# A hybrid decoder layer in fp32r on one core: where the attention of the later token tiles stands among the steps of the FFN

## The chip, the cores and the metric

One NeuronCore of a Trainium2 chip runs the whole program. The metric is device time in microseconds of one execution. The engines are named as in the profile: PE (TensorE matmul), PEld (its weight loads), DVE (VectorE), ACT (ScalarE), POOL (GpSimd) and SP (SyncE, which here issues every DMA).

## The reference, cut to what matters

One layer over 2048 positions with 1024 channels, all in float32:

```python
h = rmsnorm(x, attn_pre_norm);  qkv = h @ w_qkv
# group A: 4 heads of differential softmax attention (two maps, bias, causal) -> 512 columns
# group B: 8 heads of stick-breaking attention, 64 wide:
z = q @ k.T * 0.125
log_beta = log_sigmoid(z);  log_1mb = where(strict, log_sigmoid(-z), 0)
between = lax.cumsum(log_1mb, axis=3, reverse=True) - log_1mb
a = where(strict, exp(log_beta + between), 0);  o = rmsnorm(a @ v, sb_norm)
x = x + rmsnorm(concat(A, B) @ w_o, attn_post_norm)
h = rmsnorm(x, ffn_pre_norm)
u = causal_depthwise_conv(h @ w_up, conv_w, conv_b)     # 3 taps, 2 x 2816 columns
gate, val = split(u)
x = x + rmsnorm((gelu(gate) * val) @ w_down, ffn_post_norm)
```

## The kernel before

**Split arithmetic.** Every fp32 operand of a matmul is split into a high part rounded to fp32r and the rest; a product is three matmuls (high by high, high by low, low by high). A weight tile is split once on chip: `split` makes the high part on ACT or DVE (L477, L476) and the low part on POOL or DVE (L478, L480). Split w_up and w_down tiles are stored to DRAM (`wud`, `wdd`) and loaded again in split form for later token tiles. w_o is split for token tile 0 without a store, split again for tile 1 and stored (`wod`), and loaded in split form (512 KB a tile instead of 256 KB) for tiles 2 and 3.

**Stages.** First come the q/k/v projection in four passes and the differential attention. Then, for four token tiles of 512 positions, the stick-breaking attention (`sb_stream`) runs beside the rest of the projection and beside the FFN of earlier token tiles. The attention is a stream of 80 units: 8 for token tile 0, 16 for tile 1, 24 for tile 2 and 32 for tile 3. A unit is one head, one token tile and one 512-wide chunk of keys; `front` does its four row blocks (a matmul `z` L997, two sigmoids on ACT L1003 and L1005, one scan on DVE L1011, one product on POOL or DVE L1015 and L1017), and `tstep` transposes (L1029), splits (`hi` L485, `lo` L1036) and multiplies by v (L1052). So every unit has four scans, 320 in all.

The FFN of token tile t is `ffn_head(t)` (44 `up` steps of 24 matmuls, L1298, each with its convolution, and three of four rounds of `down`, L1351) and `ffn_tail(t)`: the output projection of the next tile `wo(t+1)` (L1218), the last round of `down`, and `h2(t+1)`, which transposes the normalised rows (L1274) into the operand `fh` of the next `up`. Between the last matmul of `wo(t+1)` and the first `up` of tile t+1 lies a chain for each of four row blocks: scale and square the projection (L1234, L1236), the reciprocal root on POOL (L402), add the residual loaded into one of two `xr` buffers (L1250), store x1 (L1253), square it (L1255), scale it (L1258), transpose (L1274), make `fh` (L1276 on ACT, L1278 on DVE). The end of `down` adds its partial sums (L1365), squares (L1373), scales (L1385), adds x1, loaded again from DRAM through the same two `xr` buffers (L1387 on POOL or L1389 on DVE), and stores the output.

**The order.** `Plan` lists the operations with a priority: the planned time `plan.now` at which the step that issues them was written, less a lead. `run` then walks through a model of the engines and always takes, for each engine that is free, the ready operation of lowest priority value whose buffers are free. What comes out is one fixed order for each engine. `merge` mixes two streams of steps in proportion to their matmul cost, and `until(sb, t, n)` hands out the attention up to the n-th unit of token tile t. Nothing keeps an operation of later priority from going first when it is ready and the earlier one is not. Weights are asked for ten tiles ahead (`AHEAD`), into five buffers `W`.

The last lines of `layer_kernel` set the mix:

```python
run(merge(until(sb, 1, 2), qkv_steps(3, 2, 8)))
ffn_switch()
run(merge(until(sb, 1, 5), wo(0)))
run(merge(until(sb, 1, 8), h2(0)))
head = list(ffn_head(2))
run(merge(until(sb, 2, 4), ffn(0)))
run(merge(until(sb, 3, 8), ffn(1)))
run(merge(until(sb), head[:-5]))
run(chain(head[-5:], ffn_tail(2), ffn(3)))
```

Of the kernel before, what the change touches and what calls it, by code (L numbers as in the profile page):

```python
# [276 lines left out]
def layer_kernel(  # L277
# [18 lines left out]
    x1d = [dram.tile([P, D], F32, name=f"x1d{i}") for i in range(NB)]  # L296
    wud = dram.tile([2 * NFT * 2, P, 1024], F32, name="wud")
    wdd = dram.tile([NFT * 2, P, 1024], F32, name="wdd")
    wod = dram.tile([KD * 2, P, 1024], F32, name="wod")
    fd = dram.tile([4, 384], F32, name="fd")  # L300

    ident = const.tile([P, P], F32, name="ident")
# [852 lines left out]
    def weight(n):  # L1155
        kind, a, b = key = jobs[n]
        w = buf("W")
        flat = lambda: f32(w.t).rearrange("p a n -> p (a n)")
        home = {"u": wud, "d": wdd, "o": wod}[kind][a * 2 + b if kind != "o" else b * 2 + a]
        if key in wstore:  # L1160
            wbufs[n] = w, (load(flat, home, 1 << 19, (w,), (wstore[key],), lead=0.0, what="wload"),)
            return
        raw = buf("raw2")
        if kind == "u":
            src = up_src[:, b * 4:(b + 1) * 4, a * P:(a + 1) * P]
            rv = lambda: raw.t.rearrange("p (k n) -> p k n", k=4)
        else:
            src = w_down[0, a * P:(a + 1) * P, b * 512:(b + 1) * 512] if kind == "d" else \
                wo_src[:, b, a * 512:(a + 1) * 512]
            rv = lambda: raw.t  # L1170
        o = load(rv, src, 1 << 18, (raw,), lead=0.0, what="wraw")
        ds = split(lambda: raw.t, lambda: w.t[:, 0, :], lambda: w.t[:, 1, :], 512, (o,), (raw, w), 0.0)

        first = key not in wseen
        wseen.add(key)
        if not first or (kind == "u" and b == 0) or (kind == "d" and a % 2 == 0):
            wstore[key] = op(SPE, 0, lambda: nc.sync.dma_start(home, flat()), ds, (w,), 0, 1 << 19, "wstore")
        wbufs[n] = w, ds

# [15 lines left out]
    def wo(t):  # L1195
        st = {}

        def begin():
            st["mix"] = []
            for k in range(KD):  # L1200
                b = buf("fh")
                assert len(mixs[k, t]) == (2 if k < 4 else 1)
                st["mix"].append((b, load(lambda b=b: f32(b.t), mixd[t][k], 1 << 19, (b,), mixs[k, t], lead=20e3,
                                          what="mixload")))

        def part(h, k, js):
            if (h, k) not in st:
                st[h, k] = take("o", h, k)
            w, wd = st[h, k]
            mb, ml = st["mix"][k]  # L1210
            for j in js:
                if k == 0:
                    st["ps", h, j] = buf("pf")
                ps = st["ps", h, j]

                def go(j=j, ps=ps):
                    for n, (a, b) in enumerate(((0, 0), (0, 1), (1, 0))):
                        nc.tensor.matmul(ps.t, mb.t[:, a, j * P:(j + 1) * P], w.t[:, b, :],  # L1218
                                         start=(k == 0 and n == 0), stop=(k == KD - 1 and n == 2))
                prev = st.get((h, j, "last"))  # L1220
                st[h, j, "last"] = op("PE", 3 * c_mm(512), go, [ml, *wd] + ([prev] if prev else []), (ps, mb, w),
                                      what="wo")
                if k == KD - 1:
                    evac(h, j, ps, st[h, j, "last"])

        def evac(h, j, ps, last):
            if h == 0:
                x1b[t, j] = buf("x1")
                st["ss", j] = small("ws"), []
            x1 = x1b[t, j]  # L1230
            ss, sq = st["ss", j]
            junk = buf("junk")
            xh = lambda c: x1.t[:, c * 512:(c + 1) * 512]
            sq.append(op("DVE", c_dvp(512), lambda: nc.vector.tensor_tensor(  # L1234
                xh(h), ps.t, gain_t[:, h * 512:(h + 1) * 512], ALU.mult), (last, mem["ga"]), (ps, x1)))
            sq.append(op("ACT", c_act(512, True), lambda: nc.scalar.activation(  # L1236
                junk.t[:, 0:512], ps.t, AF.Square, accum_out=ss.t[:, h:h + 1]), (last,), (ps, junk, ss)))
            if h == 0:
                return
            b = 4 * t + j  # L1240
            s2 = small("ws")
            o = op("DVE", 70, lambda: nc.vector.tensor_tensor(ss.t[:, 2:3], ss.t[:, 0:1], ss.t[:, 1:2], ALU.add), sq,
                   (ss,))
            r, o = rs_ops(lambda: ss.t[:, 2:3], D, 1, (o,), (ss,), "ws")
            os_ = []
            for c in range(2):
                xb = buf("xr")
                lx = load(lambda xb=xb: xb.t, x2[b * P:(b + 1) * P, c * 512:(c + 1) * 512], 1 << 18, (xb,), lead=20e3,
                          what="xload")
                os_.append(op("DVE", c_dvs(512), lambda c=c, xb=xb: nc.vector.scalar_tensor_tensor(  # L1250
                    xh(c), xh(c), r.t[:, 0:1], xb.t, ALU.mult, ALU.add), (o, lx), (x1, r, xb)))
            flat = lambda: x1.t
            x1store[b] = op(SPE, 0, lambda: nc.sync.dma_start(x1d[b], flat()), os_, (x1,), 0, 1 << 19, "x1store")  # L1253
            junk2 = buf("junk")
            o = op("ACT", c_act(D, True), lambda: nc.scalar.activation(  # L1255
                junk2.t, flat(), AF.Square, accum_out=s2.t[:, 0:1]), os_, (x1, junk2, s2))
            r2, o = rs_ops(lambda: s2.t[:, 0:1], D, 1, (o,), (s2,), "ws")
            xdone[t, j] = op("DVE", c_copy(D), lambda: nc.vector.tensor_scalar(  # L1258
                flat(), flat(), r2.t[:, 0:1], None, ALU.mult), (o, x1store[b]), (x1, r2))

        yield 0.0, begin
        for h in range(2):
            for k, js in rank(KD):
                yield 3 * len(js) * c_mm(512), lambda h=h, k=k, js=js: part(h, k, js)

    def h2(t):

        def step(k):
            ps, hb = buf("pf"), buf("fh")
            xs = [x1b[t, j] for j in range(4)]  # L1270

            def tr():
                for j in range(4):
                    nc.tensor.transpose(ps.t[:, j * P:(j + 1) * P], xs[j].t[:, k * P:(k + 1) * P], ident)  # L1274
            o = op("PE", 436, tr, [xdone[t, j] for j in range(4)], (*xs, ps), what="h2T")
            o1 = op("ACT", c_act(512) + 95, lambda: nc.scalar.activation(  # L1276
                hb.t[:, 0, :], ps.t, AF.Identity, scale=g_ffn[:, k:k + 1]), (o, mem["gffn"]), (ps, hb))
            o2 = op("DVE", c_dvp(512), lambda: nc.vector.scalar_tensor_tensor(  # L1278
                hb.t[:, 1, :], ps.t, g_ffn[:, k:k + 1], f32(hb.t[:, 0, :]), ALU.mult, ALU.subtract), (o1,), (ps, hb))
            h2b[t][k] = hb, (o1, o2)  # L1280

        for k in range(KD):
            yield 436, lambda k=k: step(k)

    ysv, halod, gts, yas, yss = {}, {}, {}, {}, {}

# [47 lines left out]
    def down(t, r, h):  # L1334
# [24 lines left out]
        def evac(j, ps, last):  # L1359
# [19 lines left out]
                   (ss,))  # L1379
            rr, o = rs_ops(lambda: ss.t[:, 2:3], D, 1, (o,), (ss,), "ws")  # L1380
            for c in range(2):
                yc, xb = yas[t, c, j][0], buf("xr")
                cs = slice(c * 512, (c + 1) * 512)
                lx = load(lambda xb=xb: xb.t, x1d[rb][:, cs], 1 << 18, (xb,), (x1store[rb],), lead=20e3, what="x1load")
                oc = op("DVE", c_dvs(512), lambda yc=yc, cs=cs: nc.vector.scalar_tensor_tensor(  # L1385
                    yc.t, yc.t, rr.t[:, 0:1], mem["gain"][:, cs], ALU.mult, ALU.mult), (o, mem["gf"]), (yc, rr))
                oc = op("POOL", c_pool(512), lambda yc=yc, xb=xb: nc.gpsimd.tensor_tensor(  # L1387
                    yc.t, yc.t, xb.t, ALU.add), (oc, lx), (yc, xb)).alt(
                    "DVE", c_dvs(512), lambda yc=yc, xb=xb: nc.vector.tensor_tensor(yc.t, yc.t, xb.t, ALU.add))  # L1389
                op(SPE, 0, lambda yc=yc, cs=cs: nc.sync.dma_start(out2[rb * P:(rb + 1) * P, cs], yc.t), (oc,), (yc,),  # L1390
                   0, 1 << 18, "out")

# [3 lines left out]
    def ffn_head(t):  # L1396
        for r, (a, b) in enumerate(ROUNDS):
# [3 lines left out]
            if r + 1 < len(ROUNDS):  # L1401
                for h in range(2):
                    yield from down(t, r, h)

    def ffn_tail(t):
        if t + 1 < NTT:
            yield from wo(t + 1)
        for h in range(2):
# [49 lines left out]
    op(None, 0, sb_open, users("k", "v", "q", "thi", "tlo", "mo", "ot", "os", "sq", "mix", "sm", "z", "o", "w", "a"))  # L1458
    sb = sb_stream()
    plan.slack = 2500.0  # L1460
    run(merge(until(sb, 1, 2), qkv_steps(3, 2, 8)))
    ffn_switch()
    run(merge(until(sb, 1, 5), wo(0)))
    run(merge(until(sb, 1, 8), h2(0)))
    head = list(ffn_head(2))
    run(merge(until(sb, 2, 4), ffn(0)))
    run(merge(until(sb, 3, 8), ffn(1)))
    run(merge(until(sb), head[:-5]))
    run(chain(head[-5:], ffn_tail(2), ffn(3)))
    plan.run()  # L1470
# [36 lines left out]
```

## Time and profile before

| | |
|---|---|
| median of 2 runs | 3154.66 us (3153.62 to 3155.71) |
| the profiled execution | 3157.89 us, span 3156.1 us |
| mean granted TensorE clock | 0.980 |
| PE busy | 3006.2 us (95%) |
| DVE busy | 2125.1 us (67%) |
| ACT busy | 1451.7 us (46%) |
| POOL busy | 649.4 us (21%) |
| DMA | 630.47 MB, 200 GB/s over the span |

The span is the time from the first to the last instruction of the profiled execution; the device time has a little around it. Busy shares are of the span. A matmul's own duration is longer than the distance between two of them, so PE can read as wholly busy while it doesn't run at its densest; the number of matmuls in a stretch tells more than its busy time.

### The profile page before, as it was taken

The page shows a single profiled execution, that of the slowest core. Times are in us where ns is not written, and L with a number is a line of the kernel's source. Part 1 is how long each engine was busy: PE and PEld are TensorE (multiplying, and loading weights), DVE is VectorE, ACT ScalarE, POOL GpSimd, SP SyncE. Part 2 cuts the span into 40 slices and gives each one's busy share as a digit, 9 for nine tenths or more (in the row PEclk, how much of TensorE's full clock was granted, in tenths as well). Part 3 has the DMA queues.
Part 4 walks back from the last instruction along what each step waited for, and adds up shares of the span by engine and source line. Part 5 has one row for each costly group of instructions (what it writes and reads, how often), then busy time and mean ns, then how long its engine had stood idle before and what let it go on. Part 6 is the DMA issues. An engine that isn't in the chain of part 4 may idle for free.

```text
span 3156.1 us, 47203 instructions
## 1 busy us (share of the span) xinstructions
PE 3006.2 (95%) x16840; PEld 2590.9 (82%) x16840; DVE 2125.1 (67%) x4273; ACT 1451.7 (46%) x2861; POOL 649.4 (21%) x831
## 2 busy tenths in 40 slices
PE   7999999999998899999889999998999999899997
PEld 7899999999997688888777887876888888678885
DVE  4657877679577676676586878778767777352334
ACT  4434545445344555455355556454655555222112
POOL 1011001002022332222331333333233222100000
PEclk9999999999999899999999999999999999999998
DMA  7776748565576555656676666676655555665665
GB/s 250 254 221 187 212 138 243 152 205 166 161 221 207 170 183 184 197 184 201 233 239 227 210 215 209 210 236 204 208 177 178 173 172 191 217 214 193 194 193 161
DMA packets 344256, 630.47 MB, mean 200 GB/s; under 512 B 29680, under 2 KB 200404, under 8 KB 335828
## 3 DMA queue, kind: packets, MB, share of 16 engines
q1 hardware_dynamic: 344020, 627.45, 62.4%
q8 instruction: 133, 2.18, 0.3%
q14 instruction: 103, 0.84, 0.1%
HBM read 449.07 MB, written 178.26 MB: 199 GB/s over the span
## 4 chain that ended last, share of the span: by engine, by line
PE 77%; DVE 10%; DMA 3%; ACT 2%; issue 2%; POOL 1%; SPq 0%; POOLq 0%; DVEq 0%; ACTq 0%
PE pf L1298 28%; PE pf L1351 13%; PE g L623 9%; PE g L620 5%; PE pf L1218 4%; PE o L1052 3%; PE z L726 3%; PE zt L997 3%; PE zt L1029 3%; DVE gm L1011 2%; PE t L744 2%; PE o L906 1%; PE o L911 1%; PE o L905 1%; DVE ya L1385 1%
## 5 line engine op out<-in xcount | busy, mean ns | idle before, releaser
L1298 PE MATMUL pf<-fh,W 128*128 128x512 f32 x4224 | 1041.7, 395 | 0.1
L1298 PEld LDWEIGHTS pf<-fh,W 128*128 128x128 f32 x4224 | 784.7, 189 | 164.7 <-DVE fh L1278 0.4
L1351 PE MATMUL pf<-W,gt 128*128 128x512 f32 x2112 | 532.3, 396 | 11.5 <-DVE x L1234 3.8
L1351 PEld LDWEIGHTS pf<-W,gt 128*128 128x128 f32 x2112 | 390.0, 189 | 97.0 <-DVE ya L1365 6.8
L623 PE MATMUL g<-hT,big 128*128 128x256 f32 x3072 | 446.8, 288 | 11.0 <-DVE st L642 5.7
L1015 POOL TENSOR_TENSOR be<-be,gm 128x512 f32<-128x512 f32 (+3 forms) x218 | 292.1, 1350 | 725.2 <-DVE gm L1011 419.6
L623 PEld LDWEIGHTS g<-hT,big 128*128 128x128 f32 x3072 | 407.3, 193 | 22.3 <-DVE st L642 7.7
L1011 DVE TENSOR_TENSOR_SCAN gm<-gm,gm 128x513 f32<-128x513 f32 x192 | 277.2, 1463 | 34.5 <-ACT gm L1003 33.6
L1036 DVE TENSOR_TENSOR lo<-zt,hi 128x512 fp32r<-128x512 f32 (+1 forms) x320 | 192.5, 605 | 119.6 <-ACT hi L485 118.0
L1309 DVE SCALAR_TENSOR_TENSOR fy<-pf,cw,fy 128x511 f32<-128x511 f32 x176 | 131.2, 745 | 210.1 <-ACT fy L1305 206.5
L485 ACT CAST hi<-zt 128x512 fp32r<-128x512 f32 (+3 forms) x250 | 130.2, 523 | 258.4 <-PE zt L1029 256.0
L1305 ACT ACTIVATE fy<-pf,cw 128x512 f32<-128x512 f32 x176 | 137.0, 778 | 210.6 <-PE pf L1298 210.6
L620 PE MATMUL g<-big,hT 128*128 128x256 f32 x1536 | 227.1, 289 | 5.3 <-DVE st L662 1.9
L620 PEld LDWEIGHTS g<-big,hT 128*128 128x128 f32 x1536 | 206.3, 194 | 11.3 <-DVE st L662 2.2
L1003 ACT ACTIVATE gm<-zt 128x512 f32<-128x512 f32 (+2 forms) x320 | 172.8, 540 | 82.6 <-PE zt L1000 44.5
L477 ACT CAST W<-raw 128x512 fp32r<-128x512 f32 x193 | 119.6, 623 | 190.7 <-PE pf L1298 68.9
L1029 PE MATMUL zt<-ident,be 128*128 128x128 f32 x1088 | 178.3, 279 | 24.5 <-POOL be L1015 8.9
L402 POOL TENSOR_TENSOR sm<-sm,neghalf 128x2 f32<-128x2 f32 (+1 forms) x72 | 71.3, 991 | 618.4 <-DVE sm L400 590.0
L1218 PE MATMUL pf<-W,fh 128*128 128x512 f32 x768 | 191.0, 402 | 7.7 <-DMA fh<-mixd 6.9
L997 PE MATMUL zt<-k,q 128*128 128x512 f32 (+3 forms) x640 | 183.1, 381 | 12.8 <-DVE lo L1036 8.8
L480 DVE TENSOR_TENSOR W<-raw,W 128x512 fp32r<-128x512 f32 x150 | 114.1, 763 | 117.6 <-ACT W L477 112.8
L1029 PEld LDWEIGHTS zt<-ident,be 128*128 128x128 f32 x1088 | 138.4, 144 | 62.6 <-POOL be L1015 10.3
(158 smaller groups left out, 4590.2 us busy)
## 6 DMA issues: line engine op xcount, KB each, us to landing
W<-wud SPq DMA_DIRECT2D x220, 512.0 KB, 3.9
W<-wdd SPq DMA_DIRECT2D x110, 512.0 KB, 4.4
hT<-hd SPq DMA_DIRECT2D x48, 1024.0 KB, 5.6
wud<-W SPq DMA_DIRECT2D x88, 512.0 KB, 4.1
raw<-in_w_up_dram SPq DMA_DIRECT2D x132, 256.0 KB, 3.3
q<-qd SPq DMA_DIRECT2D x128, 256.0 KB, 4.8
wdd<-W SPq DMA_DIRECT2D x44, 512.0 KB, 4.1
k<-kd SPq DMA_DIRECT2D x80, 256.0 KB, 3.7
```

Of the source, the lines that this page charges most:

```text
L620: nc.tensor.matmul(ps.t[:, cs], hk[:, b, c * P:(c + 1) * P], wv[:, a, k, :], start=first, stop=last)
L623: nc.tensor.matmul(ps.t[:, cs], wv[:, a, k, c * P:(c + 1) * P], hk[:, b, :], start=first, stop=last)
L997: nc.tensor.matmul(ps.t[:, 0:w], q.t[:, l, jj * P:(jj + 1) * P], kt.t[:, 0:w], start=(l == 0), stop=(l == 1 and not diag))
L1003: o1 = op("ACT", c_act(w), lambda: nc.scalar.activation(gm.t[:, 0:w], ps.t[:, 0:w], AF.Sigmoid, scale=-1.0), (o,), (gm, ps), what="sig").t ...
L1011: nc.vector.tensor_tensor_scan(gr, gr, gr, 1.0 if cb is None else cb[0].t[:, 0:1], ALU.mult, ALU.bypass)
L1015: o = op("POOL", c_pool(w), lambda: nc.gpsimd.tensor_tensor(be.t[:, 0:w], be.t[:, 0:w], gm.t[:, 1:w + 1], ALU.mult), (o1, o2), (be, gm), w ...
L1029: nc.tensor.transpose(ps.t[:, jj * P:(jj + 1) * P], rows[jj][0].t[:, kb * P:(kb + 1) * P], ident)
L1036: ol = op("DVE", c_dvp(n), lambda: nc.vector.tensor_tensor(lo.t[:, sl], ps.t[:, sl], f32(hi.t[:, sl]), ALU.subtract), (oh,), (ps, hi, lo), ...
L1218: nc.tensor.matmul(ps.t, mb.t[:, a, j * P:(j + 1) * P], w.t[:, b, :], start=(k == 0 and n == 0), stop=(k == KD - 1 and n == 2))
L1298: nc.tensor.matmul(ps.t, wv[:, a, k % 4, :], h2b[t][k][0].t[:, b, :], start=(k == 0 and i == 0), stop=(k == KD - 1 and i == 2))
L1305: o1 = op("ACT", c_act(512) + 95, lambda: nc.scalar.activation(y.t, ps.t, AF.Identity, scale=sc(2), bias=sc(3)), (last, *mem["cw"]), (ps, ...
L1351: nc.tensor.matmul(ps.t, gt.t[:, x, j * P:(j + 1) * P], w.t[:, y, :], start=(i == 0 and n == 0), stop=(m == b - 1 and n == 2))
```

## The change

Four edits of one kernel.

- `ffn_tail(0)` and `ffn_tail(1)` are run by themselves, with no attention units mixed in; they were mixed with attention as parts of `ffn(0)` and `ffn(1)`.
- The attention units are shared out anew. Up to the end of the named step there were 10 units (projection), 13 (`wo(0)`), 16 (`h2(0)`), 28 (`ffn(0)`), 56 (`ffn(1)`) and 80 (`ffn_head(2)`). Now there are 10 at the end of the projection's tile 5, 14 at its end, 19 (`wo(0)`), 24 (`h2(0)`), 40 (`ffn_head(0)`), 60 (`ffn_head(1)`) and 80 (`ffn_head(2)`).
- The operations that `evac` of `wo` issues and those of each `h2` step get a priority 30 us earlier.
- w_o is split from its raw form for every token tile; `wod`, its stores and its loads in split form are gone. For the last token tile the four x1 blocks are loaded whole into the four `x1` buffers at the start of `ffn_tail(3)`, instead of in halves through `xr`.

```diff
-        home = {"u": wud, "d": wdd, "o": wod}[kind][a * 2 + b if kind != "o" else b * 2 + a]
+        home = None if kind == "o" else {"u": wud, "d": wdd}[kind][a * 2 + b]
...
-        if not first or (kind == "u" and b == 0) or (kind == "d" and a % 2 == 0):
+        if kind != "o" and (not first or (kind == "u" and b == 0) or (kind == "d" and a % 2 == 0)):
             wstore[key] = op(SPE, 0, lambda: nc.sync.dma_start(home, flat()), ds, (w,), 0, 1 << 19, "wstore")
...
                 if k == KD - 1:
+                    now, plan.now = plan.now, plan.now - 30e3
                     evac(h, j, ps, st[h, j, "last"])
+                    plan.now = now
...
+        def soon(k):
+            now, plan.now = plan.now, plan.now - 30e3
+            step(k)
+            plan.now = now
+
         for k in range(KD):
-            yield 436, lambda k=k: step(k)
+            yield 436, lambda k=k: soon(k)
...
-                lx = load(lambda xb=xb: xb.t, x1d[rb][:, cs], 1 << 18, (xb,), (x1store[rb],), lead=20e3, what="x1load")
+                if t == NTT - 1:
+                    xb, lx = xlast[j]
+                    xv = lambda xb=xb, cs=cs: xb.t[:, cs]
+                else:
+                    xb = buf("xr")
+                    xv = lambda xb=xb: xb.t
+                    lx = load(xv, x1d[rb][:, cs], 1 << 18, (xb,), (x1store[rb],), lead=20e3, what="x1load")
...
+    xlast = []
+
+    def load_last():
+        for j in range(4):
+            rb = 4 * (NTT - 1) + j
+            xb = buf("x1")
+            xlast.append((xb, load(lambda xb=xb: xb.t, x1d[rb], 1 << 19, (xb,), (x1store[rb],), what="x1load")))
+
     def ffn_tail(t):
+        if t == NTT - 1:
+            yield 0.0, load_last
...
-    run(merge(until(sb, 1, 2), qkv_steps(3, 2, 8)))
+    run(merge(until(sb, 1, 2), qkv_steps(3, 2, 6)))
+    run(merge(until(sb, 1, 6), qkv_steps(3, 6, 8)))
     ffn_switch()
-    run(merge(until(sb, 1, 5), wo(0)))
-    run(merge(until(sb, 1, 8), h2(0)))
+    run(merge(until(sb, 1, 11), wo(0)))
+    run(merge(until(sb, 2, 0), h2(0)))
+    run(merge(until(sb, 2, 16), ffn_head(0)))
+    run(ffn_tail(0))
+    run(merge(until(sb, 3, 12), ffn_head(1)))
+    run(ffn_tail(1))
     head = list(ffn_head(2))
-    run(merge(until(sb, 2, 4), ffn(0)))
-    run(merge(until(sb, 3, 8), ffn(1)))
     run(merge(until(sb), head[:-5]))
```

## Rows read from the trace of the kernel before

**Rows 1.** The page, part 1: busy us and share of the span.

```profile
PE 3006.2 (95%) x16840; PEld 2590.9 (82%) x16840; DVE 2125.1 (67%) x4273; ACT 1451.7 (46%) x2861; POOL 649.4 (21%) x831
```

**Rows 2.** Busy time by stage: us, PE, PEld, DVE, ACT, POOL, clock, DMA, GB/s.

```profile
842.00:1017.00 175.00, 155.11 (x1142) 144.31 (x1141) 117.76 (x214) 83.13 (x207) 40.01 (x85) 0.96 0.74 221
1017.00:1061.00 44.00, 44.00 (x188) 35.92 (x188) 19.67 (x27) 15.32 (x31) 4.36 (x7) 0.97 0.47 149
1061.00:1104.00 43.00, 30.53 (x151) 23.09 (x149) 41.84 (x72) 28.61 (x64) 23.59 (x33) 0.80 0.64 206
1104.00:1497.00 393.00, 391.58 (x1819) 322.98 (x1818) 271.96 (x385) 219.58 (x386) 108.15 (x114) 1.00 0.58 189
1497.00:1557.00 60.00, 56.01 (x247) 45.45 (x248) 28.29 (x35) 20.75 (x46) 10.87 (x15) 0.94 0.69 244
1557.00:1618.00 61.00, 46.19 (x202) 37.13 (x201) 55.40 (x88) 31.96 (x70) 29.58 (x35) 0.86 0.69 228
1618.00:2095.00 477.00, 465.79 (x2225) 380.17 (x2223) 374.23 (x546) 264.42 (x476) 151.87 (x189) 1.00 0.66 219
2095.00:2150.00 55.00, 53.48 (x259) 44.07 (x258) 34.70 (x45) 21.45 (x47) 13.25 (x24) 1.00 0.62 208
2150.00:2202.00 52.00, 42.31 (x197) 32.66 (x196) 48.67 (x72) 28.52 (x62) 22.61 (x33) 0.89 0.71 241
2202.00:2676.00 474.00, 473.89 (x2292) 390.58 (x2290) 353.02 (x508) 253.84 (x450) 136.43 (x180) 1.00 0.55 178
2676.00:2731.00 55.00, 48.05 (x207) 38.57 (x206) 9.95 (x19) 7.46 (x18) 2.64 (x3) 0.94 0.57 200
2731.00:2773.00 42.00, 30.18 (x133) 23.58 (x131) 28.97 (x54) 17.13 (x37) 11.02 (x15) 0.89 0.79 263
2773.00:3110.00 337.00, 337.00 (x1485) 278.50 (x1484) 123.24 (x237) 65.39 (x95) 1.29 (x1) 1.00 0.61 198
3110.00:3156.00 46.00, 23.33 (x103) 18.83 (x101) 21.76 (x36) 7.82 (x19) 7.50 (x7) 0.78 0.45 138
```

**Rows 3.** The scans L1011 alone in some of these stages: us, DVE busy (count).

```profile
842.00:1017.00 175.00, 49.03 (x53) 0.96 0.74 221
...
1061.00:1104.00 43.00, 12.77 (x12) 0.80 0.64 206
1104.00:1497.00 393.00, 44.22 (x38) 1.00 0.58 189
...
1618.00:2095.00 477.00, 113.18 (x87) 1.00 0.66 219
...
2202.00:2676.00 474.00, 128.17 (x96) 1.00 0.55 178
```

**Rows 4.** The chain that ended last, around `wo(3)` and after it: start, us, what.

```profile
2700.19 4.43 DMA fh<-mixd
...
2732.46 5.70 DMA xr<-in_x_dram
...
2742.02 6.98 DMA W<-wdd
...
2759.14 3.05 DVE ya L1385 x3
...
2766.18 3.08 DVE ya L1385 x3
```

**Rows 5.** The same chain in `wo(1)`: start, us, what.

```profile
1536.46 3.91 DMA wod<-W
1540.37 1.30 POOL W L478
```

**Rows 6.** The page, part 5: two costs of a weight split (busy, mean ns).

```profile
L477 ACT CAST W<-raw 128x512 fp32r<-128x512 f32 x193 | 119.6, 623 | 190.7 <-PE pf L1298 68.9
L480 DVE TENSOR_TENSOR W<-raw,W 128x512 fp32r<-128x512 f32 x150 | 114.1, 763 | 117.6 <-ACT W L477 112.8
```

**Rows 7.** The same chain after the last matmul: start, us, what.

```profile
3148.41 4.04 DMA xr<-x1d
```

More of the change, by code (lines that the diff above doesn't have):

```diff
@@ L298, in layer_kernel @@
     wdd = dram.tile([NFT * 2, P, 1024], F32, name="wdd")
-    wod = dram.tile([KD * 2, P, 1024], F32, name="wod")
     fd = dram.tile([4, 384], F32, name="fd")
@@ L1381, in evac @@
             for c in range(2):
-                yc, xb = yas[t, c, j][0], buf("xr")
+                yc = yas[t, c, j][0]
                 cs = slice(c * 512, (c + 1) * 512)
-                lx = load(lambda xb=xb: xb.t, x1d[rb][:, cs], 1 << 18, (xb,), (x1store[rb],), lead=20e3, what="x1load")
+                if t == NTT - 1:
[5 more added lines that the diff above has]
+                    lx = load(xv, x1d[rb][:, cs], 1 << 18, (xb,), (x1store[rb],), lead=20e3, what="x1load")
                 oc = op("DVE", c_dvs(512), lambda yc=yc, cs=cs: nc.vector.scalar_tensor_tensor(
                     yc.t, yc.t, rr.t[:, 0:1], mem["gain"][:, cs], ALU.mult, ALU.mult), (o, mem["gf"]), (yc, rr))
-                oc = op("POOL", c_pool(512), lambda yc=yc, xb=xb: nc.gpsimd.tensor_tensor(
-                    yc.t, yc.t, xb.t, ALU.add), (oc, lx), (yc, xb)).alt(
-                    "DVE", c_dvs(512), lambda yc=yc, xb=xb: nc.vector.tensor_tensor(yc.t, yc.t, xb.t, ALU.add))
+                oc = op("POOL", c_pool(512), lambda yc=yc, xv=xv: nc.gpsimd.tensor_tensor(
+                    yc.t, yc.t, xv(), ALU.add), (oc, lx), (yc, xb)).alt(
+                    "DVE", c_dvs(512), lambda yc=yc, xv=xv: nc.vector.tensor_tensor(yc.t, yc.t, xv(), ALU.add))
                 op(SPE, 0, lambda yc=yc, cs=cs: nc.sync.dma_start(out2[rb * P:(rb + 1) * P, cs], yc.t), (oc,), (yc,),
```

## The prediction

> **What bounds the kernel now.** I read the page first, then a table of all engines cut at the kernel's own stages, then the same table for the scans alone, and last the chain of waits where that table shows a loss. PE is the engine to watch: 95% busy, against 67% for DVE [rows 1]. But 95% is a mean. In `ffn_head(3)` (2773 to 3110), where no attention is left, 1485 matmuls take 337.00 us, 0.227 us each, with no idle time; in the three heads with attention PE is busy for 391.58 of 393, 465.79 of 477 and 473.89 of 474 us [rows 2]. The losses lie between the heads. In the four stretches from the last matmul of `wo` to the next first `up` (43, 61, 52 and 42 us) PE is busy for 30.53, 46.19, 42.31 and 30.18 us, and in the first three DVE is nearly full: 41.84, 55.40 and 48.67 us [rows 2]. There PE waits for the chain from `evac` to `h2`, while DVE shares its time between that chain and the attention's scans. The fourth stretch, after `wo(3)`, has no attention left and still takes 42 us. There the chain shows loads into `xr` (5.70 us) and, ahead of the last steps of x1 and `fh`, two groups of three L1385 of the finished token tile (3.05 and 3.08 us) [rows 4]. Smaller losses: the first stage (155.11 busy of 175), `wo(1)`, and the 46 us at the end, of which PE works 23.33 [rows 2].
>
> So this is a PE-bound kernel with seams, and the change works on the seams. A seam is worth its length less what PE does in it.
>
> **The price of attention.** Counting scans, four a unit, I get 38 in `ffn_head(0)`, 87 in head 1 and 96 in head 2 [rows 3]. Over the bare head's 337 us that is (393-337)/38 = 1.47, (477-337)/87 = 1.61 and (474-337)/96 = 1.43 us a scan [rows 2, 3], all of a scan's share of PE, switches and small waits included. I take 1.5, and 1.43 for head 2, where most units are as they were. On DVE a scan with its splits and products costs (353.02-123.24)/96 = 2.4 us.
>
> **Part 1: attention moved forward.** All 320 scans still run; what counts is where. Up to 1017 there were 53 (10 units by plan, three run ahead), and 4 more units now belong there: 16 scans x 1.5 = 24, so that stage goes from 175 to 199 us. The bounds: 4 us if they fill the 20 us in which PE was idle, and 53 us at the stage's own 175/53 = 3.3 us a scan. I take the heads' price because DVE has room: 117.76 + 16 x 2.4 = 156 of 199 us, the 78% of head 1 [rows 2, 3]. In `wo(0)` some 6 scans instead of 1 make 44 into 51 us. In the stretch after it there were 12 scans in 43 us with DVE full; if the chain goes first I expect 36 us (next part) with 7 scans. `up(0)` then starts at 842 + 199 + 51 + 36 = 1128, instead of 1104, with 82 scans done instead of 66: 24 us spent, 16 scans gained, worth 24. This front is a wash.
>
> Head 0 must reach unit 40, scan 160: 78 scans x 1.5 + 337 = 454 us, to 1582. DVE would hold 271.96 + 40 x 2.4 = 368 us there, 81%: above head 1's 78%, where the price was 1.61. At that price it would be 9 us more, which goes into the range. The loads of q, k and v move forward with the units on SP's queue; DMA was 0.58 busy in this head and 0.55 in head 2 with 96 scans [rows 2, 3], so they fit.
>
> **Part 2: bare tails, with the chain in front.** The nearest row is the stretch after `wo(3)`, bare already: 42 us. Its `down` is 96 matmuls, 22 us, so PE idles because the chain is longer. With priorities 30 us earlier, x1 and `fh` no longer stand behind the 3.05 and 3.08 us of L1385 [rows 4]: 36 us. The loads through two `xr` buffers stay as they are. They carry a lead of 20 us already, and the chain's stores and loads now go ahead of weight loads on SP, behind which one wait of 6.98 us for W stands now [rows 4]; five W buffers cover that, and if they don't it costs those 7 us a tail. What is put back is L1385, POOL's sums and the output stores of the finished tile: nobody waits for these except the buffers `ya`, next used a quarter of a head later. The bounds of the chain are 30 us (the 22 us of `down` and some 8 for the transposes and their `fh`) and the 42 of now. I take 36 in all four places.
>
> The `wo` parts of tails 0 to 2 take 60, 55 and 55 us; `wo(0)` did its 188 matmuls in 44.00 [rows 2]. Without attention I take 48 for each, 4 us for starting. So a tail is 48 + 36 = 84 us. The planner takes what is ready, so some later attention still runs in the idle gaps. By DVE there is room for (36 - 28.97)/2.4 = 3 scans a tail [rows 2]; I count these as free in tails 0 and 1.
>
> Going on from 1582: tail 0 to 1666 (163 scans done); head 1 to unit 60, 77 scans x 1.5 + 337 = 453, to 2119; tail 1 to 2203; head 2, 77 x 1.43 + 337 = 447, to 2650; tail 2 to 2734; head 3 to 3071.
>
> TensorE's clock speaks against bare tails. Where PE idled, the granted clock was lower: 0.80, 0.86 and 0.89 in the three stretches with attention and 0.89 in the bare one, against 1.00 in the heads [rows 2]. So the attention's matmuls didn't hold it up, and I add nothing. [...]
>
> **Part 3: w_o split each time.** For tiles 2 and 3, 16 tiles each, a split costs ACT 0.623 us and DVE 0.763 us at most [rows 6]: 10 and 12 us in a `wo`. Cover: in `wo(3)` DVE was busy for 9.95 of 55 us [rows 2], and without attention `wo(2)` is alike. `wo(0)` took the raw way throughout and lost nothing, so I take nothing. The other bound is `wo(1)`, also raw: PE busy 56.01 of 60, 4 us idle; twice that is 8 us. The change removes 16 stores of 512 KB in `wo(1)`, which keep W buffers occupied (3.91 us for one on the chain, then a split on POOL) [rows 5], and halves 32 loads. That is in the 48.
>
> **Part 4: x1 of the last tile.** After the last matmul, two loads of x1 of some 4 us stand on the chain, each behind a sum that frees `xr` [rows 7]. Loaded ahead they are gone, and what is late next is DVE's scaling and adding: I take 7 us off 46, 39. Bounds 0 and 8. The four loads wait for `x1` buffers, which `h2(3)` freed a whole head earlier, so nothing queues behind them on SP.
>
> **The sum.** 3071 + 39 = 3110 us of span against 3156, 46 less. The profiled execution had 3157.89, 3.2 above the median: 3154.66 - 46 = 3109 us, 1.5% faster. About 2% (63 us, so 3092 to 3218) is what a measurement of this kernel can tell from no change.
>
> **The rivals.**
> - *The seams close wholly* (3080, 0.25). For it: the tails' loss is all chain. With a chain of 30 us instead of 36 in four places (-24), and the front's 16 scans filling part of PE's 20 idle us (-5), it is 3080. Against: the two `xr` buffers remain.
> - *DVE takes the place* (3149, 0.15). For it: at 81% head 0 has the highest mean load. If every scan up to unit 40 costs 0.33 us more (78 + 16 + 5 scans x 0.33 = 33) and W waits cost 7 us in one tail, it is 3149. Against: head 1's price of 1.61 at 78%.
> - *The tails aren't bare* (3130, 0.08). If the planner, which knows no barrier, goes on putting scans into DVE ahead of `down`'s part of the tail, the chains stay near 42 and 50 us: some 21 us more.
> [...]
> - *Slower* (3229, 0.07): the projection starves. Its evacuations on DVE stand behind 10 units per four tiles instead of six, and so do the FFN's after it. It decides from the point at which 16 scans don't fit into the first stage: at 3.3 us a scan there (+29), and the first stage's PE loss, 20 of 175 us or 11%, all through head 0 (+50), in the stretch after `wo(0)` (+6), and as late starts of 12 us in `wo(0)` and both bare tails (+35), it is 3229.
>
> **How the numbers follow.** The sum as worked out has 0.42, with a range of its own of 3092 to 3128: 9 us for head 0, 8 for the splits, the chain's 3 either way. The range 3070 to 3160 leaves out the slower case, the tail of the DVE case and the lowest part of the fastest, under 2 in 10. Faster by over 2% is the first rival, 0.25; slower by over 2% is the last, 0.07; within it 0.68.
>
> **What would show it.** Right: the stretches from `wo`'s last matmul to the next `up` at about 36 us, L1258 and L1278 ahead of L1385 there; three scans or so in tails 0 and 1; `up(0)` later than before (near 1128); head 0 near 454 us with no more than 3% of PE idle; no load of x1 on the chain after the last matmul. Wrong: a stretch that stays above 45 us, idle time of PE in the projection put down to DVE, waits of `wo` for L480 or L478 in tiles 2 and 3, or a head 0 above 465 us.

## The result and the profile after

The changed kernel takes 3121.91 us (median of 2 runs, 3121.15 to 3122.68) against 3154.66: 0.9896 of the kernel before, with a 95% interval of 0.9854 to 0.9939. Run again beside further runs of the kernel before, it had 0.9881 (0.9866 to 0.9895). The forecast was 3109, with a range of 3070 to 3160. The total came out as forecast in kind and 13 us off in size. Which part of the change made the gain did not come out as forecast.

The table by stage answers to [rows 2]. Its columns are the same: stretch, us, then busy time and count of PE, PEld, DVE, ACT and POOL, the granted clock, DMA share and GB/s. The cuts lie at the same places of the program: projection, `wo(0)`, chain, head 0, `wo(1)`, chain, and so on.

```profile
842.00:1040.00 198.00, 175.53 (x1239) 161.61 (x1238) 143.97 (x248) 101.76 (x251) 55.08 (x112) 0.93 0.71 215
1040.00:1097.00 57.00, 56.94 (x273) 46.56 (x272) 39.38 (x60) 27.59 (x57) 14.20 (x18) 0.99 0.48 147
1097.00:1133.00 36.00, 22.67 (x118) 17.70 (x119) 34.53 (x57) 22.59 (x50) 18.27 (x27) 0.86 0.64 201
1133.00:1587.00 454.00, 444.85 (x2130) 364.73 (x2129) 363.96 (x485) 271.26 (x495) 166.25 (x189) 1.00 0.54 177
1587.00:1640.00 53.00, 49.10 (x219) 39.20 (x218) 31.20 (x41) 19.38 (x41) 18.51 (x19) 1.00 0.48 163
1640.00:1683.00 43.00, 35.66 (x169) 29.38 (x168) 35.41 (x62) 24.97 (x56) 19.14 (x24) 0.92 0.73 248
1683.00:2130.00 447.00, 439.77 (x2080) 360.12 (x2079) 340.52 (x507) 242.77 (x427) 119.09 (x151) 1.00 0.66 220
2130.00:2177.00 47.00, 46.23 (x211) 38.09 (x210) 23.11 (x35) 18.14 (x38) 6.84 (x9) 1.00 0.59 188
2177.00:2223.00 46.00, 40.50 (x197) 32.02 (x195) 41.82 (x75) 28.23 (x62) 19.70 (x26) 0.96 0.71 242
2223.00:2664.00 441.00, 441.00 (x2099) 363.14 (x2099) 304.35 (x448) 209.23 (x375) 106.58 (x142) 1.00 0.56 181
2664.00:2710.00 46.00, 44.68 (x195) 36.30 (x195) 15.82 (x27) 12.45 (x26) 1.85 (x2) 1.00 0.50 176
2710.00:2743.00 33.00, 27.23 (x124) 21.17 (x123) 22.31 (x44) 16.14 (x36) 7.11 (x10) 0.97 0.89 302
2743.00:3081.00 338.00, 337.58 (x1487) 278.92 (x1486) 128.84 (x245) 65.91 (x95) 6.04 (x5) 1.00 0.64 205
3081.00:3121.00 40.00, 23.53 (x104) 19.00 (x102) 21.40 (x35) 7.82 (x19) 10.31 (x9) 0.82 0.35 121
```

The scans alone (now L1010), which answer to [rows 3]:

```profile
1133.00:1587.00 454.00, 97.94 (x76) 1.00 0.54 177
1587.00:1640.00 53.00, 9.65 (x7) 1.00 0.48 163
1640.00:1683.00 43.00, 2.55 (x2) 0.92 0.73 248
1683.00:2130.00 447.00, 87.01 (x71) 1.00 0.66 220
2130.00:2177.00 47.00, 3.58 (x4) 1.00 0.59 188
2177.00:2223.00 46.00, 8.58 (x7) 0.96 0.71 242
2223.00:2664.00 441.00, 93.94 (x71) 1.00 0.56 181
```

What to see: tails 0, 1 and 2 (`wo` and the chain after it together) went from 121, 107 and 97 us to 96, 93 and 79. Scans still run in the "bare" tails, 9 and 11 of them, against 15 and 18 before. The heads give and take: head 0 grew by 61 us for 38 scans more, head 2 shrank by 33 us for 25 fewer. The end went from 46 to 40 us. The table by itself suggests that the bare tails did it. The experiments say otherwise.

### The profile page after: what moved, and what is told of

Same layout as the page of the kernel before. It is cut to its first block, busy times and chain, and to the rows that moved or that the text cites. A ratio compares the mean times of both kernels' runs of the same rounds, so it can differ in the third digit from the quotient of the medians.

```text
span 3120.8 us, 47246 instructions
## 1 busy us (share of the span) xinstructions
PE 2996.1 (96%) x16840; PEld 2584.5 (83%) x16840; DVE 2142.2 (69%) x4305; ACT 1454.7 (47%) x2881; POOL 654.4 (21%) x833
## 4 chain that ended last, share of the span: by engine, by line
PE 78%; DVE 11%; issue 3%; ACT 2%; DMA 1%; POOL 1%; SPq 0%; DVEq 0%; ACTq 0%; POOLq 0%
PE pf L1304 28%; PE pf L1357 13%; PE g L622 9%; PE g L619 5%; PE pf L1217 5%; PE o L1051 3%; PE z L725 3%; PE zt L996 3%; PE zt L1028 3%; DVE gm L1010 3%; PE t L743 2%; PE o L905 1%; PE o L910 1%; PE o L904 1%; DVE be L1016 1%
## 5 line engine op out<-in xcount | busy, mean ns | idle before, releaser
L1357 PE MATMUL pf<-W,gt 128*128 128x512 f32 x2112 | 525.2, 394 | 12.0 <-DVE fy L1316 6.7
L1014 POOL TENSOR_TENSOR be<-be,gm 128x512 f32<-128x512 f32 (+3 forms) x208 | 275.0, 1330 | 770.4 <-DVE gm L1010 369.3
L1010 DVE TENSOR_TENSOR_SCAN gm<-gm,gm 128x513 f32<-128x513 f32 x192 | 271.0, 1431 | 24.8 <-ACT gm L1002 24.5
L476 ACT CAST W<-raw 128x512 fp32r<-128x512 f32 x218 | 135.5, 623 | 216.2 <-PE pf L1357 70.1
L479 DVE TENSOR_TENSOR W<-raw,W 128x512 fp32r<-128x512 f32 x176 | 138.2, 788 | 131.8 <-ACT W L476 121.2
L996 PE MATMUL zt<-k,q 128*128 128x512 f32 (+3 forms) x640 | 182.9, 381 | 25.5 <-DVE lo L1035 12.5
L1217 PE MATMUL pf<-W,fh 128*128 128x512 f32 x768 | 183.4, 394 | 3.7 <-ACT halo L1324 1.9
L477 POOL TENSOR_TENSOR W<-raw,W 128x512 fp32r<-128x512 f32 x86 | 130.3, 1515 | 263.9 <-ACT W L476 128.8
```

Of the source, the lines that this page charges most:

```text
L479: "DVE", c_dvs(n), lambda: nc.vector.tensor_tensor(lo(), raw(), f32(hi()), ALU.subtract))
L996: nc.tensor.matmul(ps.t[:, 0:w], q.t[:, l, jj * P:(jj + 1) * P], kt.t[:, 0:w], start=(l == 0), stop=(l == 1 and not diag))
L1010: nc.vector.tensor_tensor_scan(gr, gr, gr, 1.0 if cb is None else cb[0].t[:, 0:1], ALU.mult, ALU.bypass)
L1014: o = op("POOL", c_pool(w), lambda: nc.gpsimd.tensor_tensor(be.t[:, 0:w], be.t[:, 0:w], gm.t[:, 1:w + 1], ALU.mult), (o1, o2), (be, gm), w ...
L1357: nc.tensor.matmul(ps.t, gt.t[:, x, j * P:(j + 1) * P], w.t[:, y, :], start=(i == 0 and n == 0), stop=(m == b - 1 and n == 2))
```

## The experiments

Ratios are to the kernel before, run beside each experiment on the same chip. Each has an interval of about 0.0015 either way (5 us), so a difference of two ratios is known to some 7 us.

**Without the chain's priority.**

```diff
-                    now, plan.now = plan.now, plan.now - 30e3
                     evac(h, j, ps, st[h, j, "last"])
-                    plan.now = now
...
-            yield 436, lambda k=k: soon(k)
+            yield 436, lambda k=k: step(k)
```

> The changed kernel without the earlier priority of the chain (evac of wo and the h2 steps at their own planned time). Theory A (the priority clears the chain): the four stretches from the last matmul of wo to the next up go from 36, 43, 46 and 33 us back towards 42 and more, 15 to 25 us in sum, so 3137 to 3147 us. Theory B (the tails got shorter because they are bare; in the trace after, L1397 still stands ahead of L1279, so the priority reorders little): 3122 to 3127 us.

Measured: 3140.81 us, ratio 0.9947 (0.9931 to 0.9964), so 21 us slower than the changed kernel's 0.9881 (0.0066 x 3158). The stretches after `wo(1)`, `wo(2)` and `wo(3)`:

```profile
1644.00:1694.00 50.00, 38.44 (x176) 31.11 (x175) 42.54 (x70) 26.34 (x57) 19.25 (x25) 0.86 0.70 236
2182.00:2231.00 49.00, 41.92 (x191) 33.10 (x190) 44.17 (x77) 28.62 (x63) 22.72 (x27) 0.89 0.69 230
2719.00:2759.00 40.00, 28.91 (x125) 23.17 (x124) 28.02 (x53) 16.58 (x36) 10.81 (x14) 0.87 0.75 259
```

They take 50, 49 and 40 us instead of 43, 46 and 33, and the one after `wo(0)` takes 41 instead of 36: some 22 us in sum, as much as the whole loss. DVE in order of time shows how, after `wo(3)`; columns are start, us, line, operation. Without the priority, a group of three L1390 (the scaling of the finished tile, L1385 of before) runs ahead of the last of the four L1257 of x1, and the other five ahead of `fh` (L1277):

```profile
2745.33 3.08 DVE L1390 SCALAR_TENSOR_TENSOR ya<-ya,ws,gfpost 128x512 f32<-128x512 f32 x3
2748.33 1.75 DVE L1257 TENSOR_SCALAR x<-x,ws 128x1024 f32<-128x1024 f32 x1
...
2751.72 3.75 DVE L1390 SCALAR_TENSOR_TENSOR ya<-ya,ws,gfpost 128x512 f32<-128x512 f32 x4 [0.66 <-POOL ws L401]
2755.39 3.42 DVE L1277 SCALAR_TENSOR_TENSOR fh<-pf,g_ffn,fh 128x512 fp32r<-128x512 f32 x5
```

In the changed kernel x1 (L1259) is done first, all eight `fh` (L1279) of DVE run in one go, and one group of three L1397 (the same scaling) is left between them:

```profile
2733.90 0.75 DVE L1259 TENSOR_SCALAR x<-x,ws 128x1024 f32<-128x1024 f32 x1
...
2736.17 3.08 DVE L1397 SCALAR_TENSOR_TENSOR ya<-ya,ws,gfpost 128x512 f32<-128x512 f32 x3
...
2739.77 5.71 DVE L1279 SCALAR_TENSOR_TENSOR fh<-pf,g_ffn,fh 128x512 fp32r<-128x512 f32 x8
```

After `wo(1)` and `wo(2)` it is alike: four of the eight scalings still precede the first `fh` of DVE, and all eight without the priority. Theory A holds.

**Tails merged with attention again.**

```diff
-    run(merge(until(sb, 2, 16), ffn_head(0)))
-    run(ffn_tail(0))
-    run(merge(until(sb, 3, 12), ffn_head(1)))
-    run(ffn_tail(1))
+    run(merge(until(sb, 2, 16), ffn(0)))
+    run(merge(until(sb, 3, 12), ffn(1)))
```

> The changed kernel with the attention merged through the tails again: the same units up to the end of ffn(0) and ffn(1), but spread over head and tail. Theory A (chain priority does it; the planner fills the gaps in any case): within 5 us of 3122. Theory B (bare tails do it): tails 0 and 1 take 10 to 15 us more each for the same scans, 3137 to 3150 us.

Measured: 3116.33 us, ratio 0.9869 (0.9855 to 0.9884), no slower than the changed kernel. Theory B, which asked for 3137 us or more, falls.

**w_o stored and loaded in split form, as before.**

```diff
-        home = None if kind == "o" else {"u": wud, "d": wdd}[kind][a * 2 + b]
+        home = {"u": wud, "d": wdd, "o": wod}[kind][a * 2 + b if kind != "o" else b * 2 + a]
...
-        if kind != "o" and (not first or (kind == "u" and b == 0) or (kind == "d" and a % 2 == 0)):
+        if not first or (kind == "u" and b == 0) or (kind == "d" and a % 2 == 0):
```

> The changed kernel with w_o stored in split form in wo(1) and loaded in that form in wo(2) and wo(3), as before. Prediction's reading (the stores hold W buffers in wo(1), the splits are hidden): 3 to 8 us more, 3125 to 3130, all of it in wo(1). Rival (the 32 added splits cost DVE time that the chains of tails 1 and 2 want): 3 to 8 us less, 3114 to 3119.

Measured: 3141.81 us, ratio 0.9952 (0.9937 to 0.9967), 22 us slower than the changed kernel. The sign is the prediction's, but the size is nearly three times the upper end of what I had expected, and it is not all in `wo(1)`. `wo(1)` and the chain after it take 58 and 56 us instead of 53 and 43. `wo(2)`, `wo(3)` and the chains behind them, which now load 512 KB a tile, take 51, 51, 51 and 36 us instead of 47, 46, 46 and 33:

```profile
2134.00:2185.00 51.00, 50.68 (x235) 41.81 (x234) 23.30 (x32) 15.98 (x36) 8.70 (x11) 1.00 0.72 247
2185.00:2236.00 51.00, 41.60 (x192) 33.19 (x190) 45.23 (x75) 27.66 (x61) 24.31 (x28) 0.88 0.73 246
2674.00:2725.00 51.00, 45.54 (x192) 36.87 (x192) 7.69 (x15) 5.00 (x13) 0.55 (x1) 0.97 0.69 242
```

In `wo(3)` PE waits once for such a load, 4.7 us.

**Only the stores put back.**

```diff
+        if kind == "o" and not first and key not in ostored:
+            ostored.add(key)
+            op(SPE, 0, lambda: nc.sync.dma_start(wod[b * 2 + a], flat()), ds, (w,), 0, 1 << 19, "wstore")
         wbufs[n] = w, ds
```

> The changed kernel with the 16 stores of split w_o in wo(1) put back, but never loaded: wo(2) and wo(3) still split from the raw form. It leaves the result alone and adds 8.4 MB of stores. If the 17 us that the split each time is worth come from the stores (they stand on SP in front of the chain's loads and hold W buffers): 10 to 17 us slower than the changed kernel, all in wo(1) and the chain after it (43 to 53 us or more). If they come from the loads of 512 KB in wo(2) and wo(3): 0 to 5 us slower.

Measured: 3132.29 us, ratio 0.9910 (0.9894 to 0.9927), 9 us slower than the changed kernel; its profiled execution has a span of 3133.3 us, 12.5 more. `wo(1)` and the chain after it:

```profile
1588.00:1646.00 58.00, 55.18 (x258) 44.31 (x256) 35.93 (x43) 22.24 (x49) 21.09 (x26) 1.00 0.69 248
1646.00:1702.00 56.00, 42.40 (x186) 34.55 (x187) 49.46 (x77) 29.81 (x65) 24.96 (x29) 0.84 0.64 219
```

So the stores alone make tail 0 114 us long, as with stores and loads together, instead of 96. Of these 18 us 9 come back in head 1, which takes 438 us instead of 447: attention has moved, with 17 scans in tail 0 instead of 9 and 62 in head 1 instead of 71. Tails 1 and 2 are within 3 us of the changed kernel's (48, 45, 46 and 36 us), so the other 13 us of the run before this one stand where split w_o is loaded.

I had expected the stores to stand on SP in front of the chain's own loads. The trace shows the delay earlier, inside `wo(1)`. SP issues the last load of raw w_o at 1632.13, right behind four stores (in the changed kernel at 1620.51), and DVE, whose order is fixed, stands idle for 5.33 us until it lands:

```profile
1627.40 4.68 SPq L1180 DMA_DIRECT2D wod<-W  x4
1632.13 0.45 SPq L395 DMA_DIRECT2D raw<-in_w_o_dram  x1
1637.07 0.43 DVE L476 CAST W<-raw 128x512 fp32r<-128x512 f32 x1 [5.33 <-DMA raw<-in_w_o_dram]
...
1648.45 1.26 DVE L1239 TENSOR_TENSOR x<-pf,bias_t 128x512 f32<-128x512 f32 x2
...
1651.10 1.42 DVE L1255 SCALAR_TENSOR_TENSOR x<-x,ws,xr 128x512 f32<-128x512 f32 x2
```

The weight splits (L476, then L480) and scans that follow come so late that the first `evac` of `wo`'s second half (L1239) starts at 1648.45, after the last matmul of `wo(1)`. SP issues the next loads of x at 1651.88, as soon as that last line has freed `xr`. In the changed kernel the same `evac` (L1235) starts 2.7 us before the last matmul ends, and the x1 line follows at once:

```profile
1637.23 1.29 DVE L1235 TENSOR_TENSOR x<-pf,bias_t 128x512 f32<-128x512 f32 x2 [1.37 <-PE pf L1217]
...
1639.85 1.41 DVE L1251 SCALAR_TENSOR_TENSOR x<-x,ws,xr 128x512 f32<-128x512 f32 x2
```

In the kernel's order a store also keeps its W buffer, which can push the next split back as well. How much is due to the buffers, to the stores' place on SP and to the bytes was not separated.

**x1 of the last tile through `xr` again.**

```diff
-                if t == NTT - 1:
+                if False:
                     xb, lx = xlast[j]
...
-        if t == NTT - 1:
-            yield 0.0, load_last
```

> The changed kernel with x1 of the last token tile loaded in halves through the two xr buffers again. Prediction's reading: the end after the last matmul is 6 to 7 us longer, 3128 to 3129 us. Rival (DVE's scaling and adding bounds the end by itself): 0 to 2 us more.

Measured: 3129.6 us, ratio 0.9908 (0.9894 to 0.9923); the span of its profiled execution is 3129.0, 8.2 us more than the changed kernel's. The chain of waits has the two loads again:

```profile
3116.59 3.83 DMA xr<-x1d
...
3121.23 4.08 DMA xr<-x1d
```

The prediction's reading holds.

**The changed kernel again.**

> The changed kernel itself, beside the same runs of the kernel before as the next three. Every theory: a ratio to the kernel before of 0.9896, as it was, within 0.002.

Measured: 3122.36 us, ratio 0.9881 (0.9866 to 0.9895), within the stated 0.002.

**The whole order of before, the other edits kept.**

```diff
-    run(merge(until(sb, 1, 2), qkv_steps(3, 2, 6)))
-    run(merge(until(sb, 1, 6), qkv_steps(3, 6, 8)))
+    run(merge(until(sb, 1, 2), qkv_steps(3, 2, 8)))
     ffn_switch()
...
-    run(ffn_tail(1))
+    run(merge(until(sb, 1, 5), wo(0)))
+    run(merge(until(sb, 1, 8), h2(0)))
     head = list(ffn_head(2))
+    run(merge(until(sb, 2, 4), ffn(0)))
+    run(merge(until(sb, 3, 8), ffn(1)))
```

> The changed kernel with the order of the kernel before: attention shared out as before and mixed through the tails; the chain's priority, the split of w_o each time and the early x1 stay. Prediction's reading (the bare tails and the attention moved forward carry most of the gain): 15 to 25 us slower than the changed kernel. Theory from the runs so far (chain priority 16 us, split 17 us, x1 4 us already make more than the 33 us of gain, and bare tails cost 8): within 6 us of the changed kernel, or faster by up to 6.

Measured: 3122.16 us, ratio 0.9881 (0.9866 to 0.9895), the same as the changed kernel, where the prediction's reading asked for 15 to 25 us more. `wo(1)` and the chain after it, with attention mixed in as before:

```profile
1496.00:1544.00 48.00, 48.00 (x222) 39.71 (x221) 27.58 (x41) 19.55 (x42) 9.39 (x13) 1.00 0.58 194
1544.00:1587.00 43.00, 37.55 (x181) 30.89 (x180) 36.25 (x64) 26.19 (x58) 16.25 (x19) 0.92 0.73 244
```

48 and 43 us, against 60 and 61 before [rows 2] and 53 and 43 after. The chains behind `wo(2)` and `wo(3)` take 44 and 35 us, and tail 1 holds 22 scans. To within the 7 us, the order of the attention is worth nothing here; the chain is as short with attention merged into the tail as without.

**The front of before alone.**

```diff
-    run(merge(until(sb, 1, 2), qkv_steps(3, 2, 6)))
-    run(merge(until(sb, 1, 6), qkv_steps(3, 6, 8)))
+    run(merge(until(sb, 1, 2), qkv_steps(3, 2, 8)))
...
-    run(merge(until(sb, 1, 11), wo(0)))
-    run(merge(until(sb, 2, 0), h2(0)))
+    run(merge(until(sb, 1, 5), wo(0)))
+    run(merge(until(sb, 1, 8), h2(0)))
```

> The changed kernel with the attention only at the front as before (10, 13 and 16 units at the ends of the projection, wo(0) and h2(0)); the head of token tile 0 then has 24 units up to unit 40, the tails stay bare. Prediction's reading (moving attention forward is a wash up to the first up, and takes load off DVE in head 0): the first up starts 20 to 30 us earlier, head 0 takes 35 to 55 us more, in sum 5 to 15 us slower than the changed kernel. Rival (the crowded projection costs more than it gives back later): up to 10 us faster.

Measured: 3119.17 us, ratio 0.9869 (0.9854 to 0.9883). The first `up` starts at 1109 and `wo(1)` at 1579, 24 and 9 us earlier than in the changed kernel: head 0 takes 15 us more, not the 35 to 55 that I had expected, and what follows some 5 more. So it is a wash, as the prediction had it; the 5 to 15 us slower that I expected of this run did not come, and the 3 us faster are within the interval.

**The chain's priority alone, on the kernel before.**

```diff
+                    now, plan.now = plan.now, plan.now - 30e3
                     evac(h, j, ps, st[h, j, "last"])
+                    plan.now = now
...
-            yield 436, lambda k=k: step(k)
+            yield 436, lambda k=k: soon(k)
```

> The kernel before with the chain's earlier priority alone. If the three working parts simply add (priority about 19 us, as when it was taken out of the changed kernel): 0.994 of the kernel before, 3140 us where that takes 3159. If the stores of split w_o still hold the chain up in tail 0, and attention in the tails fills DVE, it gives less: 5 to 12 us. If it is the whole gain by itself: 30 us or more.

Measured: 3143.14 us, ratio 0.9950 (0.9935 to 0.9964), 16 us faster than the kernel before. That is between the first two expectations. The stretches after `wo(2)` and `wo(3)` come down to 43 and 34 us, from 52 and 42, but the one after `wo(1)` stays at 55:

```profile
1557.00:1612.00 55.00, 41.25 (x188) 32.90 (x187) 48.98 (x81) 27.70 (x64) 30.95 (x38) 0.91 0.65 220
```

With the same order of the attention and w_o split each time it was 43 (the run of the whole order of before): with the stores there, the priority can't clear it. After `wo(0)` it is 42 us, against 43 before: there the priority alone does nothing.

**The finished tile's work put off behind `fh`.**

```diff
+            def finish(extra=()):
...
+            late.append(finish)
...
             yield from h2(t + 1)
+            yield 0.0, lambda: [late.pop(0)(h2b[t + 1][KD - 1][1]) for _ in range(4)]
```

> The changed kernel with the end of a finished token tile (sum of squares, root, L1385's scaling, the add of x1, the output store) made to wait for the last fh of the next tile, for token tiles 0 to 2. The prediction had it that the chain's priority puts x1 and fh ahead of this work; the trace after shows it still ahead of L1279. If that work costs the chain its DVE time: the stretches after wo(1), wo(2) and wo(3) get 3 to 5 us shorter each, 3108 to 3114 us where the changed kernel takes 3122. If DVE only fills gaps with it while the chain waits for loads and stores of x1: within 3 us of the changed kernel; and if putting it off burdens the start of the next head: up to 5 us slower.

Measured: 3122.85 us, ratio 0.9893 (0.9877 to 0.9910), no gain. No L1397 stands ahead of DVE's `fh` any more, and yet the first `fh` after `wo(3)` starts 29 us after the last matmul, against 30. The L1397 that the trace of the changed kernel still shows there cost it little.

**Three `xr` buffers.**

```diff
-                    ("fh", KD), ("W", 5), ("raw2", 3), ("xr", 2), ...
+                    ("fh", KD), ("W", 5), ("raw2", 3), ("xr", 3), ...
```

> The changed kernel with three xr buffers instead of two (the room for it comes from one identity matrix instead of two and 20 instead of 24 small tiles of the attention). If the loads of x through two buffers set the pace of the four row blocks in the chain, as I held against a chain of 30 us: the stretches after wo get 3 to 6 us shorter in all four places, 3102 to 3112 us where the changed kernel takes 3122. If DVE or ACT sets the pace: within 4 us of the changed kernel.

The room for the third buffer comes from one identity matrix instead of two and 20 instead of 24 small tiles. Measured: 3123.85 us, ratio 0.9895 (0.9881 to 0.9910), no gain, though the stretches after `wo(1)`, `wo(2)` and `wo(3)` are shorter by 4 us each:

```profile
1647.00:1686.00 39.00, 34.64 (x172) 28.12 (x171) 33.64 (x61) 23.71 (x52) 19.55 (x21) 0.96 0.72 240
2186.00:2228.00 42.00, 38.09 (x188) 30.64 (x187) 37.65 (x64) 26.91 (x61) 21.72 (x27) 0.96 0.72 250
2716.00:2745.00 29.00, 26.85 (x130) 21.22 (x128) 19.87 (x43) 15.56 (x35) 6.31 (x10) 1.00 0.93 324
```

From the first `wo` on, both profiled executions take 2080 us. So the 12 us are given back, in the heads that follow: head 1 takes 452 us instead of 447, head 2 443 instead of 441, and the last head is 5 us longer to its last matmul. There PE now waits for its weights (engine, line, waited for, us, times, longest), and DMA is at 0.93 in the stretch before it, against 0.89. Why head 1 is longer stays open.

```profile
PE pf L1304 <- DMA W<-wud: 3.4, 2, 3.2
```

The front of this kernel was 7 us later by the first `wo` as well; whether that, or any of the rest, comes from the room made for the buffer wasn't tried.

**Both order edits undone in part.** The front of before, and tails merged up to units 40 and 60:

```diff
...
+    run(merge(until(sb, 1, 2), qkv_steps(3, 2, 8)))
     ffn_switch()
...
+    run(merge(until(sb, 1, 5), wo(0)))
+    run(merge(until(sb, 1, 8), h2(0)))
+    run(merge(until(sb, 2, 16), ffn(0)))
+    run(merge(until(sb, 3, 12), ffn(1)))
```

> The changed kernel with the front of the kernel before (10, 13 and 16 units) and the tails merged with attention again, head and tail 0 up to unit 40, head and tail 1 up to unit 60; the chain's priority, the split each time and the early x1 stay. Each of the two order edits taken alone gave 0.9869 of the kernel before, the changed kernel 0.988 to 0.990. If the two add: 0.984 to 0.986, 3107 to 3114 us where the kernel before takes 3158. If the order of the attention simply doesn't matter within a few us, as the order of before showed (0.9881): 0.986 to 0.989, 3114 to 3124 us.

Measured: 3117.15 us, ratio 0.9868 (0.9852 to 0.9885). The two do not add. It is 0.0013 below the changed kernel's second measurement, within the intervals, so no version here beats the changed kernel clearly.

## Why the prediction was right in sum, and where it was wrong

- **The front** was right: 198 us against 199, 57 against 51 in `wo(0)`, 36 against 36 after it, `up(0)` at 1133 against 1128, and no gain by itself. The 36 needed both edits: 43 us before, 42 with the priority alone, 41 with the attention moved but no priority.
- **Head 0** was right: 454 us against 454, with 76 scans against 78. The price of 1.5 us a scan came out at (454-337)/76 = 1.54. Heads 1 and 2 took 447 and 441 us against 453 and 447, with 71 scans each instead of 77. The loads of the moved units showed nowhere: PE has no wait for them in head 0, where its waits, 9.1 us in sum, are all for DVE.
- **The bare tails were the step that failed.** Part 2 took the stretch after `wo(3)`, "bare already: 42 us", as what a tail becomes when attention leaves it, and "without attention I take 48 for each". With the attention back in the tails nothing is lost (0.9869 and 0.9881): the chains stay as short, 43, 44 and 35 us. That attention only fills gaps behind the chain fits this; it is argued. Nor were the tails bare, with 9 and 11 scans where the sum had three each. That was the rival "the tails aren't bare", in its premise and, with 21 us more in tails 0 and 1, in its price; what it left out is that the scans are then missing in heads 1 and 2, 12 of them and 12 us.
- **The chain's priority** was right in sign and in most of its mechanism: x1 (L1259) stands ahead of all of the scaling but for one after `wo(1)`, while DVE's `fh` (L1279) passes only about half of it. It is worth 21 us when taken out and 16 when put in alone. In size, 36 us in all four places met 36, 43, 46 and 33; the third is beyond the 45 us that the prediction had named as a sign of being wrong. Tails 0 and 1, at 96 and 93 us instead of 84, and the front are 26 us too long; heads 1 and 2 and tail 2 gave 17 back. With 2 in the last head and at the end that is the miss of 11 us in the span (3121 against 3110); the rest of the 13 is how far the two profiled executions lie from their medians.
- **w_o split each time** was mis-sized. I counted it at nothing beyond a share "in the 48", and bounded it by PE's idle time in `wo(1)`, which leaves out the chain behind; taken out it costs 22 us, 9 of them by the stores alone, the rest where `wo(2)` and `wo(3)` load twice the bytes. The wait on the chain for one store [rows 5] was a sign of it. The splits themselves were hidden, as forecast: among PE's waits in `wo(1)`, `wo(2)` and `wo(3)`, 3.7, 0.8 and 1.3 us in sum, none is for a split.
- **x1 ahead** was right: 40 us at the end against 39, 8 us of span when undone.
- **The bound of the chain** held back by "two xr buffers" was right for the stretch (4 us each) and wrong for the total: the heads behind give the 12 us back. Of the 5 in the last head, 3.4 are a wait for W, the kind that the prediction had named with its 6.98 us [rows 4]; the others stay open.
- The singles sum to 21 + 22 + 8 = 51 us against a gain of 37 in the same runs. They are not additive: stored w_o and the missing priority lengthen the same stretch after `wo(1)`. It takes 61 us in the kernel before, 55 with the priority put in, 50 in the changed kernel without the priority, and 43 in the changed kernel.
- **Clock.** The stretches that got shorter also ran at a higher granted clock, 0.92, 0.96 and 0.97 against 0.86, 0.89 and 0.89 [rows 2], with 2, 7 and 0 scans in them. So the granted clock rose in the tails instead of falling. The 0.68 for a time within 2% holds 0.03 for tails slowed by a falling clock; no run shows such a loss. With bare tails the lowest clock of these stretches in any table here is 0.84 (only the stores put back).
- **The sum** came close partly by luck. It gave the new order of the attention a share in the gain, which the runs put at nothing, and the end of the stores and split loads next to none, which they put at 22 us; the two errors work against each other.

## What to carry to other kernels

When a change has several parts, the stage that shortens does not tell which part shortened it; undo each part by itself, the scheduling edits above all, since a greedy planner refills what an order empties (9 and 11 scans in the bare tails here). In a seam between saturated stages, put the chain that opens the next stage ahead of work that nobody waits for; here that gave 16 us put in alone and cost 21 when taken out. Storing a prepared operand to reload it later can cost more than preparing it again, when the stores and the larger loads fall into such seams: 22 us here.

## What was unexpected

Sixteen stores of 512 KB that no one reads make one tail 18 us longer and the kernel 9, though the DMA share there is only 0.64 to 0.69. And a third `xr` buffer made three chains 4 us shorter each without a gain in the total: the heads behind gave it back.
